# Prompt-only modulation in the first group, a two-pair weight fold, unsaved pooling splits and reductions tied to the heads

## The chip, the cores and the metric

The kernel runs on one core of a Trainium2 chip. The metric is the device time of one execution in microseconds (us); lower is better. The time before is the median of three runs.

TensorE (PE) multiplies matrices; VectorE (DVE), ScalarE (ACT) and GpSimd (POOL) work on vectors; SyncE (SP) issues most transfers. Each engine takes its own instructions strictly in the order of the program, and so an instruction that waits holds up all that stands behind it on its engine.

## The reference

One layer of a streaming encoder, in float32, for a prompt of 2048 tokens and a sample of 64, with the model's width 1024:

```python
mod = (c_act @ w_ada + b_ada)[:, None, :]            # six vectors of 1024, for prompt and sample
sh1, sc1, gt1, sh2, sc2, gt2 = jnp.split(mod, 6, -1)
h = rmsnorm(x, g1) * (1 + sc1) + sh1
proj = h @ w_in                                       # u (pooling), q, k, v, o, gates
pool_out = pool_mixer(u, ...)                         # causal means of 2, 4, 8, 16 rows, then @ w_pool per group
hs, C, n, m = mlstm_seq(q, k, v, ig, lf, C, n, m)     # 4 heads, chunked, state carried from chunk to chunk
hs = hs * rsqrt(mean(hs * hs) + EPS) * g_head * sigmoid(o)
x = x + gt1 * (concat([pool_out, hs]) @ w_out)
h2 = rmsnorm(x, g2) * (1 + sc2) + sh2
up = h2 @ w_up                                        # then a causal convolution, a gate, and w_down
x = x + gt2 * ((silu(g) * a) @ w_down)
```

It returns both outputs and the new states.

## The kernel before

The mixer takes four groups of tokens, called here g0 to g3 (three of 512 and a last of 576 that holds the sample), and runs from 0 to some 760 us; the gated MLP takes the rest, and the change does not touch it.

A product is computed in split arithmetic: a weight and an input are each held as a high and a low part, and three passes (high by high, high by low, low by high) make one product. A weight's split costs one ACT instruction (the high part, L394) and one DVE instruction (the low part, L397). `halves` makes the list of weight units of 128x512 for the heads and the pooling projections: in g0 a unit is loaded raw (256 KB, L373), split, and the split is stored to `hl_kept` in DRAM (512 KB, L402); in g1 to g3 the finished split is loaded (512 KB, L378). The output projection's weights are loaded raw and split in each group.

A group goes through these phases: the V projection (L1129); four heads, each with a product for q, k and the gate (`gemm`, L460) beside which the recurrence of the head before it runs; the pooling projections, called U here (L460 with the same `hl` inputs); and the output projection (L460 with `mx` inputs). A head's recurrence (`lstm`) is a chain over the engines:

- PE expands the gate rows (L1293) and transposes k (L1301); DVE scales it into `kw`; PE multiplies q by k (L1319).
- PE makes the states' products from `kw` (L1334); DVE adds them up (`st`, `SP`).
- PE makes the cells (L1354, L1356); ACT and DVE gather them into `nd`; DVE, ACT and POOL work out a factor `sf` (its power on POOL, L1376); DVE scales `nd` by it.
- `end` transposes `nd` back (L1388), one head later, or for the last head within U.

Small sums over the group's rows (`ssum`) go to PE at L515 and come back through DVE copies into `scr`, which L521 needs. For the next group DVE adds squares of rows (L910).

Between these, background generators are advanced by `tick(i)` at fixed points of `gemm`, the V projection and the drains. Two are of interest. `ada(m)` computes one of the six modulation vectors without PE: for each of 16 pieces of `w_ada` (256 KB each) two DVE reductions (L210), one with the prompt's conditioning vector and one with the sample's; each is followed by a short read of the accumulator. g0 runs `ada(2)` and g1 to g3 run `ada(3)` to `ada(5)`. `weight_sums` loads 1 MB of `w_up`, makes four DVE sums (L849 to L854) and stores 1 MB to `wsum` (L855), which the MLP reads; it runs in g1 to g3. A third, `fold`, runs once, in g0: it multiplies rows of `w_out` by `w_pool` on PE (L887), copies the result (L888) and stores it as `wo_in`.

A scheduler puts the instructions of all these into one order for each engine, going by priorities and its own estimate of durations; `keep_in_program_order` pins an instruction. Transfers go out in SP's order, and a load into a buffer waits there until the buffer's last reader is done.

## Time and profile before

| | |
|---|---|
| median of 3 runs | 2160.68 us (2160.2 to 2161.01) |
| profiled execution | 2162.98 us |
| its span, from first to last instruction | 2161.2 us |
| PE busy | 2139.0 us, 99% |
| DVE, ACT, POOL busy | 1628.4, 1094.3, 248.0 us |
| granted PE clock | 0.999 |

The profiled execution's own time is 1.78 us above its span, and 2.30 us above the median of the runs shown. PE is the bound nearly all the way: what PE waits is the little that is left.

### The profile page before, as it was taken

The numbers are of one execution on the slowest core, as the hardware profiler recorded it, in microseconds if no ns is written. First come the engines' busy times: TensorE is split into PE (matmuls) and PEld (weight loads), VectorE is DVE, ScalarE is ACT, GpSimd is POOL, SyncE is SP. The second block draws the span as 40 slices with busy tenths as digits, with TensorE's granted clock in tenths as the row PEclk, the third lists the DMA queues.
The fourth block names the chain that finished last, engine by engine and source line by source line (L and its number), as shares of the span: only waits on it lengthen the run. The fifth ranks groups of instructions, "written<-read, shape, count | busy, mean of one in ns | idle before, by whom it ended". The sixth has DMA issues, their size and how long they took to land.

```text
span 2161.2 us, 37940 instructions
## 1 busy us (share of the span) xinstructions
PE 2139.0 (99%) x13488; PEld 2039.1 (94%) x13488; DVE 1628.4 (75%) x3068; ACT 1094.3 (51%) x2182; POOL 248.0 (11%) x499
## 2 busy tenths in 40 slices
PE   8999999999999999999999999999999999999998
PEld 7878988888899999999999999999999999999998
DVE  5688768767964868797967668988876597887874
ACT  4554335334333546464636445655655365565554
POOL 0000000002000101010101220100101231111112
PEclk9999999999999999999999999999999999999999
DMA  8897998988886576889967976666668675555552
GB/s 313 318 327 254 326 340 278 357 319 290 282 306 224 169 256 220 305 278 313 341 216 249 322 258 211 230 221 207 220 228 281 209 264 184 176 176 186 175 159 79
DMA packets 245862, 543.63 MB, mean 252 GB/s; under 512 B 25252, under 2 KB 68772, under 8 KB 242856
## 3 DMA queue, kind: packets, MB, share of 16 engines
q1 hardware_dynamic: 236232, 518.89, 70.7%
q10 hardware_dynamic: 9440, 22.32, 2.6%
q8 instruction: 106, 1.74, 0.3%
q14 instruction: 84, 0.69, 0.1%
HBM read 415.12 MB, written 125.99 MB: 250 GB/s over the span
## 4 chain that ended last, share of the span: by engine, by line
PE 78%; DVE 4%; DMA 3%; issue 1%; ACT 1%; SPq 0%; POOL 0%; POOLq 0%; DVEq 0%; ACTq 0%
PE mm L1599 37%; PE mm L460 16%; PE mm L2171 12%; PE mm L2047 9%; PE mm L1129 1%; DVE wt L397 1%; DMA wt<-wsum 1%; DMA raw<-w_ada 1%; DMA wsplit<-wt 1%; PE m L1354 0%; PE m L1356 0%; PE m L1334 0%; DMA wsum<-w 0%; PE m L1319 0%; DMA qs<-w_quad 0%
## 5 line engine op out<-in xcount | busy, mean ns | idle before, releaser
L1599 PE MATMUL mm<-hx,wt 128*128 128x352 f32 x5544 | 885.6, 321 | 1.3 <-DVE eg L1608 0.8
L1599 PEld LDWEIGHTS mm<-hx,wt 128*128 128x128 f32 x5544 | 879.0, 188 | 2.7 <-DVE wt L397 1.4
L460 PE MATMUL mm<-hl,wt 128*128 128x512 f32 (+2 forms) x1920 | 387.6, 357 | 0.2 <-ACT va L233 0.2
L394 ACT ACTIVATE wt<-raw 128x512 fp32r<-128x512 f32 (+3 forms) x470 | 276.9, 597 | 172.6 <-PE mm L2171 50.1
L460 PEld LDWEIGHTS mm<-hl,wt 128*128 128x128 f32 x1920 | 315.0, 189 | 43.0 <-ACT va L233 0.4
L397 DVE TENSOR_TENSOR wt<-raw,wt 128x512 fp32r<-128x512 f32 (+3 forms) x470 | 312.3, 670 | 54.4 <-ACT wt L394 51.9
L2171 PE MATMUL mm<-av,wt 128*128 128x448 f32 (+1 forms) x1632 | 262.7, 322 | 0.0
L2171 PEld LDWEIGHTS mm<-av,wt 128*128 128x128 f32 x1632 | 250.4, 188 | 11.1
L2017 DVE SCALAR_TENSOR_TENSOR x<-mm,MOD,x 128x352 f32<-128x352 f32 (+3 forms) x360 | 167.2, 502 | 78.9 <-PE mm L2171 66.2
L2047 PE MATMUL mm<-av,wt 128*128 128x352 f32 x1344 | 219.7, 323 | 0.9 <-DVE x L2017 0.7
L2047 PEld LDWEIGHTS mm<-av,wt 128*128 128x128 f32 x1344 | 215.3, 188 | 3.2 <-DVE x L2017 1.0
L1646 ACT ACTIVATE mm<-mm 128x352 f32<-128x352 f32 x196 | 87.9, 448 | 239.9 <-PE mm L1599 188.4
L460 PE MATMUL mm<-mx,wt 128*128 128x512 f32 (+1 forms) x960 | 183.0, 352 | 0.3 <-DVE scr L233 0.3
L460 PEld LDWEIGHTS mm<-mx,wt 128*128 128x128 f32 x960 | 159.4, 188 | 23.1 <-issue 0.5
L1577 DVE SCALAR_TENSOR_TENSOR ta<-ea,V,ta 128x704 f32<-128x704 f32 (+1 forms) x132 | 125.6, 952 | 63.3 <-ACT ta L1572 50.6
L1577 DVE SCALAR_TENSOR_TENSOR tg<-eg,V,tg 128x704 f32<-128x704 f32 (+1 forms) x132 | 125.7, 952 | 60.6 <-ACT tg L1572 58.2
L397 DVE TENSOR_TENSOR wt<-wt 128x512 fp32r<-128x512 f32 x196 | 132.5, 682 | 12.7 <-ACT wt L394 12.7
L394 ACT ACTIVATE wt<-wt 128x512 fp32r<-128x512 f32 x196 | 119.9, 623 | 43.4 <-DMA wt<-wsum 33.0
L1555 POOL COPY ea<-UC 128x2 f32<-128x2 f32 x66 | 32.9, 498 | 491.1 <-DVE ta L1577 389.0
L1786 ACT ACTIVATE tg<-tg 128x704 f32<-128x704 f32 (+1 forms) x66 | 52.5, 795 | 71.2 <-DVE tg L1577 71.2
L1129 PE MATMUL mm<-wt,hl 128*128 128x256 f32 (+1 forms) x576 | 71.1, 284 | 0.0
L1129 PEld LDWEIGHTS mm<-wt,hl 128*128 128x128 f32 x576 | 70.3, 190 | 0.6 <-issue 0.4
(298 smaller groups left out, 2169.3 us busy)
## 6 DMA issues: line engine op xcount, KB each, us to landing
wt<-wsplit SPq DMA_DIRECT2D x132, 512.0 KB, 4.4
raw<-w_up SPq DMA_DIRECT2D x198, 256.0 KB, 4.0
wt<-hl_kept SPq DMA_DIRECT2D x96, 512.0 KB, 6.0
wt<-wsum SPq DMA_DIRECT2D x132, 256.0 KB, 4.9
wsplit<-wt SPq DMA_DIRECT2D x66, 512.0 KB, 5.5
w<-w_up SPq DMA_DIRECT2D x44, 512.0 KB, 5.4
wsum<-w SPq DMA_DIRECT2D x22, 1024.0 KB, 4.9
Bd<-fscr ACTq DMA_DIRECT2D x56, 352.0 KB, 4.1
```

Of the source, the lines that this page charges most:

```text
L394: act.activation(u.w[:, 0, :u.n], u.raw[:, :u.n], AF.Copy)
L397: dve.tensor_tensor(out=u.w[:, 1, :u.n], in0=u.raw[:, :u.n], in1=u.w[:, 0, :u.n].bitcast(F32), op=ALU.subtract)
L460: pe.matmul(ps[bi][:, :hi - lo], U[:, a, k % 4 * P:(k % 4 + 1) * P], mv[k][:, b, lo:hi], start=(at == 0 and pi == 0), stop=(k == order[-1] ...
L1129: pe.matmul(ps[ti][:n, :cols], h[4 * kh + k4][:, b, lo:lo + n], U[:, a, k4 % 2 * cols:(k4 % 2 + 1) * cols], start=(kh == 0 and k4 == 0 and ...
L1555: pool.tensor_copy(ext[:, 0:2], UC[:, f, :])
L1577: dve.scalar_tensor_tensor(out=t[:, :E], in0=ext[:, j:j + E], scalar=wc(j, f), in1=t[:, :E], op0=ALU.mult, op1=ALU.add)
L1599: pe.matmul(bk.t[:, :FH], U[:, a, kc * P:(kc + 1) * P], Bo.at(nm, kc, b), start=(first and kc == 0 and pi == 0), stop=(kc == 3 and pi == 2 ...
L1646: act.activation(to.t[:, :FH], bk.t[:, :FH], AF.Copy)
L1786: act.activation(self.tg[:, :E], self.tg[:, :E], AF.Silu)
L2017: dve.scalar_tensor_tensor(out=x3[n][:, a:b], in0=bk.t[:, a - lo:b - lo], scalar=gt2(n, s), in1=x3[n][:, a:b], op0=ALU.mult, op1=ALU.add)
L2047: pe.matmul(bk.t[:, :FH], U[:, a, c:c + P], quad.put(op, m, b), start=(first and m == 0 and pi == 0), stop=(m == 1 and pi == 2), skip_grou ...
L2171: pe.matmul(bks[i].t[:, :hi - lo], U[:, a, k % 4 * P:(k % 4 + 1) * P], av[k][:, b, lo:hi], start=(k == 0 and (a, b) == PASSES[0]), stop=(k ...
```

## The change

Five things, of which the line numbers after the change are some 5 to 20 higher (L460 is L464, L1334 is L1351, L1354 and L1356 are L1372 and L1374, L397 is L400, L849 to L854 are L854 to L859, L515 and L521 are L520 and L526).

- `ada(2)` in g0 makes the prompt's part alone, 16 reductions in place of 32. The 16 of the sample are made in g1, g2 and g3 (6, 6 and 4), behind that group's own `ada`, and the pieces of `w_ada` are loaded again for it. All of `ada`'s reductions are pinned in program order now, where only those of `ada(2)` were.
- From g1 on, `tick(3)`, which advances `ada`, no longer comes in `gemm`, but in the head's recurrence: two steps behind the cells and four behind the scaling of `nd`. In the V projection it moves to the second half.
- `fold` uses two pairs of buffers (one pair are the state tiles `SS` and `SN`, not yet in use), loads two steps ahead, and issues its 8 loads and 8 stores of 256 KB on ACT's queue in place of SP's 4 and 4 of 512 KB.
- The pooling projections' splits are not stored: each group loads their weights raw and splits them, 8 more splits on ACT and on DVE in each of g1 to g3; 8 stores and 24 loads of 512 KB go, 24 loads of 256 KB come.
- In the last head of a group, `end` comes one step later.

```diff
-    def ada(m, quarter=None):
+    def ada(m, quarter=None, ss=(0, 1), bs=range(KD)):
-        todo = [(b, i) for b in range(KD) for i in range(2)]
+        todo = [(b, i) for b in bs for i in range(2)]
...
-        pin = tc.keep_in_program_order if m in (2,) else lambda i: i
+        pin = tc.keep_in_program_order
...
-            for s in range(2):
+            for s in ss:
...
     def halves(key, src, n):
...
+            if key < 4:
+                out.append((src[:, c:c + w], w))
+                continue
...
     def gemm(...):
...
-            if at == 4 and not quiet and not spare:
+            if at == 4 and not quiet and not spare and first_group:
                 tick(3)
...
-        for i in (1, 3):
-            tick(i)
+        tick(1)
+        if first_group:
+            tick(3)
...
         def fold():
+            first = quarter(True)
+            pairs = [[first[:, 0], first[:, 1]],
+                     [t.rearrange("p h c -> p (h c)")[:, :512] for t in (SS, SN)]]
+
+            def load(n):
+                for i, t in enumerate(pairs[n // 2 % 2]):
+                    act.dma_start(out=t, in_=w_out[n + i, :, :512])
+            load(0)
+            load(2)
+            yield
             for n in range(0, KD, 2):
-                w = quarter(True)
-                nc.sync.dma_start(out=w, in_=w_out[n:n + 2, :, :512].rearrange("n p c -> p n c"))
-                yield
-                for i in range(2):
-                    t = w[:, i]
+                for i, t in enumerate(pairs[n // 2 % 2]):
                     ps = m2_ps()
                     for gi in range(4):
                         c = slice(gi * P, (gi + 1) * P)
                         pe.matmul(ps[:, c], WPT[:, c], t[:, c], start=True, stop=True)
                     act.activation(t, ps, AF.Copy)
-                    if i == 0:
-                        yield
-                nc.sync.dma_start(out=wo_in[n:n + 2].rearrange("n p c -> p n c"), in_=w)
-                yield
+                    act.dma_start(out=wo_in[n + i], in_=t)
+                    if i == 0 and 2 <= n < KD - 2:
+                        load(n + 2)
+                    yield
...
-                    if hv == 0 and ti % 2 == 0:
+                    if hv == 1 and ti % 2 == 0:
                         tick(3)
...
+        def steps(o, n):
+            if o.g > 0:
+                for _ in range(n):
+                    tick(3)
         def lstm(o, hd, qko, va, cols, mix):
...
+            steps(o, 2)
...
+            steps(o, 4)
...
-                for _ in range(5 - len(o.segs)):
+                for _ in range(6 - len(o.segs)):
                     yield
                 end()
...
             if o.g > 0:
+                first_group.clear()
                 bg[3].append(ada(2 + o.g))
+                bg[3].append(ada(2, ss=(1,), bs=(None, (0, 1, 2), (3, 4, 5), (6, 7))[o.g]))
+                tick(3)
...
-                    bg[3].append(ada(2, quarter))
+                    bg[3].append(ada(2, quarter, (0,)))
```

Three places show how this moves instructions. A trailing x3 counts like instructions in a row; `m`, `mm` are PSUM tiles, `w` a tile of `weight_sums`, `hl` the group's normalised input, `va` the values, `RHL` the gate rows.

DVE in g2, between head 0 and the `kw` of head 1. Before, the end of the list reads

```order
L850 TENSOR_TENSOR w_4462<-w_4462 128x512
L910 TENSOR_TENSOR ssum<-ssum,mx_4364 128x576
L852 TENSOR_TENSOR w_4462<-w_4462 128x512
L854 TENSOR_TENSOR w_4462<-w_4462 128x512
L910 TENSOR_TENSOR ssum<-ssum,mx_4364 128x576
L233 TENSOR_TENSOR kw<-m_4751,CL 128x512
```

and after the change

```order
L210 ISA raw,MOD<-raw,acc,MOD 128x512
L210 ISA MOD 128x1
L854 TENSOR_TENSOR w_4480<-w_4480 128x512
L855 TENSOR_TENSOR w_4480<-w_4480 128x512
L857 TENSOR_TENSOR w_4480<-w_4480 128x512
L233 TENSOR_TENSOR kw<-m_4761,CL 128x512
```

The reduction at the top is the last of twelve that now stand between this head's cells and the next head's `kw`; before there was one.

PE in g2, from the last cell of head 2 (`m_5016`, later `m_5041`) on. Before:

```order
L1356 MATMUL m_5016<-va,at 128x129
L460 MATMUL mm<-hl_3955,wt 128x512 x3
L460 MATMUL mm<-hl_3731,wt 128x512 x3
L460 MATMUL mm<-hl_3742,wt 128x512 x3
L460 MATMUL mm<-hl_3755,wt 128x512 x3
L460 MATMUL mm<-hl_3804,wt 128x512 x3
L460 MATMUL mm<-hl_3809,wt 128x512 x3
L460 MATMUL mm<-hl_3858,wt 128x512 x3
L460 MATMUL mm<-hl_3905,wt 128x512 x3
L460 MATMUL mm<-hl_3955,wt 128x512 x3
```

After:

```order
L1374 MATMUL m_5041<-va,at 128x129
L464 MATMUL mm<-hl_3981,wt 128x512 x3
L464 MATMUL mm<-hl_3757,wt 128x512 x3
L464 MATMUL mm<-hl_3768,wt 128x512 x3
L464 MATMUL mm<-hl_3781,wt 128x512 x3
L464 MATMUL mm<-hl_3830,wt 128x512 x3
L1309 MATMUL m_5204<-RHL,E_r 128x512
L520 MATMUL m_5169<-ssum,ones_r 32x128 x4
L520 MATMUL m_5169<-ssum,ones_r 32x64
L464 MATMUL mm<-hl_3835,wt 128x512 x3
L464 MATMUL mm<-hl_3884,wt 128x512 x3
L464 MATMUL mm<-hl_3931,wt 128x512 x3
```

The sum over `ssum` now stands 15 products behind that cell; before, the row L515 stood 51 behind it, and from the cell to the states of head 3 there were 60 products, now 39.

PE and DVE in g2 at the start of U. Before, PE passed from the last cells of head 3 (`m_5221`) into products whose weights were split long before:

```order
L1354 MATMUL m_5221<-st_5193,q 128x129
L1356 MATMUL m_5221<-va,at 128x129
L460 MATMUL mm<-hl_3955,wt 128x512 x3
L460 MATMUL mm<-hl_3731,wt 128x512 x3
L460 MATMUL mm<-hl_3742,wt 128x512 x3
```

After the change the next product is U's first, and DVE, whose rows follow, splits its weight only behind the scaling of `nd`:

```order
L464 MATMUL mm<-hl_3931,wt 128x512 x3
L464 MATMUL mm<-hl_3981,wt 128x512 x3
L1374 MATMUL m_5271<-va,at 128x129
L1372 MATMUL m_5275<-st_5244,q 128x129
L1374 MATMUL m_5275<-va,at 128x129
L464 MATMUL mm<-hl_3757,wt 128x512 x3
```

```order
L233 SCALAR_TENSOR_TENSOR nd<-m_5275,CL,nd 128x129
L233 TENSOR_TENSOR sf<-nd 128x4
L233 TENSOR_TENSOR sf<-sf,CL 128x4
L233 SCALAR_TENSOR_TENSOR sf<-sf,sq 128x4
L233 TENSOR_TENSOR nd<-nd,sf 128x4x128
L400 TENSOR_TENSOR wt<-raw,wt 128x512 x5
```

So the first U product reads a weight whose split waits, on DVE, for the last cell that PE made just before it.

More of the change, by code (lines that the diff above doesn't have):

```diff
@@ L195, in load @@
                 got[i] = raw_tile()[:, :512]
-                nc.sync.dma_start(out=got[i], in_=w_ada[m - 2, i])
+                nc.sync.dma_start(out=got[i], in_=w_ada[m - 2, 2 * todo[i][0] + todo[i][1]])
         lead = 4 if quarter else 3
-        pin = tc.keep_in_program_order if m in (2,) else lambda i: i
-        cond = [[a1.tile([P, UE], F32, tag=nm, name=nm)[:, :512] for nm in two] for two in (("u", "s1"), ("s2", "acc"))]
-        for s in range(2):
+        pin = tc.keep_in_program_order
+        cond = {s: [a1.tile([P, UE], F32, tag=nm, name=nm)[:, :512] for nm in (("u", "s1"), ("s2", "acc"))[s]] for s in ss}
+        for s in ss:
             for i in range(2):
@@ L207, in ada @@
             w = got.pop(n)
-            for s in range(2):
+            for s in ss:
                 to = MOD[:, m, b, s:s + 1]
-                pin(dve.tensor_tensor_reduce(out=w if s else junk[0], in0=w, in1=cond[s][i], scale=1.0,
+                pin(dve.tensor_tensor_reduce(out=w if s == ss[-1] else junk[0], in0=w, in1=cond[s][i], scale=1.0,
                                              scalar=to if i else V[:, V_BA + m * 8 + b:V_BA + m * 8 + b + 1],
@@ L262, in tile_layer @@
     stream = []
-    hl_kept = dr.tile([32, P, 2, 512], F32, tag="hl_kept", name="hl_kept")
+    hl_kept = dr.tile([24, P, 2, 512], F32, tag="hl_kept", name="hl_kept")
     place_of = {}
@@ L448, in tile_layer @@
     quiet = []
+    first_group = [1]
     def gemm(ps, W, mv, o, ks=None, order=None, late=None, ups=(1, 3, 4, 6)):
@@ L1321, in lstm @@
                 dve.tensor_tensor(out=at[:n, lo:lo + w], in0=at[:n, lo:lo + w], in1=pq[:n, :w], op=ALU.mult)
+            steps(o, 0)
             while ends:
@@ L1340, in lstm @@
                                              in1=pv[:, ti - a, :], op0=ALU.mult, op1=ALU.add)
+            steps(o, 0)
             extra()
```

## The prediction

> **What bounds it now.** I read the page's busy times and its chain first, then PE's waits within the mixer, then stretches and single rows. The columns of the first row are busy time, share and count; the second gives the shares of the chain that ended last.

> ```profile
> PE 2139.0 (99%) x13488; PEld 2039.1 (94%) x13488; DVE 1628.4 (75%) x3068; ACT 1094.3 (51%) x2182; POOL 248.0 (11%) x499
> PE 78%; DVE 4%; DMA 3%; issue 1%; ACT 1%; SPq 0%; POOL 0%; POOLq 0%; DVEq 0%; ACTq 0%
> ```

> PE is the bound. The change gives it the same multiplications, so the time moves only by what PE stands idle. Of that the mixer has, from 10 to 770 us (line, what it waited for: total, times, longest):

> ```profile
> PE m L1334 <- DVE kw L233: 2.0, 2, 1.8
> PE m L887 <- DMA w<-w_out: 1.9, 2, 1.2
> PE mm L1388 <- DVE nd L233: 1.1, 1, 1.1
> PE m L962 <- ACT scr L960: 0.4, 1, 0.4
> PE m L521 <- ACT scr L233: 0.4, 1, 0.4
> PE mm L460 <- DVE scr L233: 0.3, 1, 0.3
> PE mm L1058 <- ACT hl L983: 0.3, 1, 0.3
> PE mm L460 <- ACT va L233: 0.2, 1, 0.2
> ```

> These are 6.6 us, 0.3% of the time: the most that the change can win, and no pooling projection or kept weight is among them. In the stretch

> ```profile
> 620.00:647.00 27.00, 26.60 (x201) 25.89 (x200) 16.13 (x41) 10.93 (x36) 2.37 (x7) 1.00 0.88 318
> ```

> PE lacks another 0.4 us of 27, in g3. A new wait, on the other hand, costs PE its whole length.

> **The change, part by part.** *The fold.* Both its waits (1.9) are for loads issued a few us ahead of use:

> ```profile
> 99.36 0.38 SPq L880 DMA_DIRECT2D w<-w_out  x1
> 104.05 1.16 PE L887 MATMUL m<-w,WPT 128*128 128x128 f32 x8 [0.74 <-DMA w<-w_out]
> ```

> Issued two steps ahead they land in time: gain 1.9 (0 to 1.9). [...] The 16 issues cost ACT some 0.38 each, 6 us beside its 49% of idle time; two of them wait for a store of the same buffer to land, a few us in which ACT's copies stand still, and PE has products to do: 0.2 (0 to 2).

> *g0's other waits.* Half its reductions leave DVE, and `end` of the last head comes behind 33 products in place of 18, 15 times 0.23 us (below) against a wait of 1.1: gain 1.1, with L521's 0.4 and the lesser `kw` wait of 0.2. The 0.4 of g3 goes with the sums that moved. Together 2.1 (1 to 2.1).

> *Four heads, `kw`.* The other `kw` wait is in g1, between head 0 and 1:

> ```profile
> 265.05 0.39 PE L1356 MATMUL m<-va,at 128*128 128x129 f32 x2
> 265.19 13.19 PE L460 MATMUL mm<-hl,wt 128*128 128x512 f32 x57
> 282.88 1.16 PE L1334 MATMUL m<-va,kw 128*128 128x129 f32 x8 [1.79 <-DVE kw L233]
> ```

> A product takes 13.19/57 = 0.231 us. From the last cell at about 265.3 PE has work until 281.1, and `kw`, 0.69 long, must start by 280.4: 15.1 us after the cell. DVE's list there is priced by these rows:

> ```profile
> 266.63 0.75 DVE L210 CUSTOM_DVE_ANT_0 junk<-raw,s,MOD 128x512 f32<-128x512 f32 x1 [3.02 <-DMA raw<-w_ada]
> 277.39 0.69 DVE L852 TENSOR_TENSOR w<-w 128x512 f32<-128x512 f32 x1
> 278.00 0.69 DVE L910 TENSOR_TENSOR ssum<-ssum,mx 128x512 f32<-128x512 f32 x1
> 279.20 0.74 DVE L210 CUSTOM_DVE_ANT_0 junk<-raw,u,V 128x512 f32<-128x512 f32 x1
> 282.13 0.69 DVE L233 TENSOR_TENSOR kw<-m,CL 128x512 f32<-128x512 f32 x1
> ```

> Four reductions with their reads run from 279.20 to 282.13: 0.73 each. A sum takes 0.61 (277.39 to 278.00). After the cell come some 1.3 for `nd`, 0.5 for `sf`, 0.75 of waiting for POOL and 0.6 for the scaling: 3.15. Before, with 10 reductions and 9 sums, that is 3.15 + 7.3 + 5.5 = 16.0 (the row says 16.9; the late piece of `w_ada` in the first row is the rest). After: 12 reductions and 7 sums in g1 heads 1 and 2, 12 and 6 in g2 head 1, 12 and 5 in g2 head 2, that is 16.2, 16.2, 15.6, 15.0 against 15.1. Waits of 1.1, 1.1, 0.5 and 0.2: 2.9 in place of 1.8. PE's cover is the same 60 products in all four. Bounds: 0 if the lists are 1 us shorter, and 3.0 more if one piece is as late as above.

> *g1, head 3.* The weight of U's first product is split on DVE behind `kw` and two more, four times 0.61, while PE has 1.9 us: 0.5; with a chance of a late reduction, 0.8 (0 to 2). In g3 the heads' cover is 126 shorter products and the lists are no longer than in g1: 0.2 (0 to 1).

> *g2, head 3.* Before, it looks so:

> ```profile
> 485.23 0.39 PE L1356 MATMUL m<-va,at 128*128 128x129 f32 x2
> 485.84 0.87 DVE L233 SCALAR_TENSOR_TENSOR nd<-m,CL,nd 128x129 f32<-128x129 f32 x3 [0.64 <-ACT nd L233]
> 489.22 0.69 DVE L233 TENSOR_TENSOR nd<-nd,sf 128x512 f32<-128x512 f32 x1 [1.19 <-POOL sf L1376]
> 489.83 0.75 DVE L910 TENSOR_TENSOR ssum<-ssum,mx 128x576 f32<-128x576 f32 x1
> 497.13 0.52 PE L515 MATMUL m<-ssum,ones_r 128*32 128x128 f32 x10
> ```

> The last cell ends at 485.5 and `ssum` is complete at 490.6, 5.1 us later; PE asks for it at 497.1. Now PE asks 15 products and one gate row later, 3.7 us. With one sum more in DVE's list, 5.7: a wait of 2.0 (1.4 to 2.5). L526 then needs copies that stand behind four reductions and two sums, 2.9 + 1.2 + 0.4 = 4.5, while PE has 0.5 and 12 products, 3.3: another 1.2 (0.8 to 1.6). Together 3.2.

> *g2, start of U.* The first product's low weight part comes behind the scaling of `nd`, and that behind the cell PE made just before. Before, the same chain ran beside 27 products:

> ```profile
> 507.45 0.39 PE L1356 MATMUL m<-va,at 128*128 128x129 f32 x2
> 507.59 6.40 PE L460 MATMUL mm<-hl,wt 128*128 128x512 f32 x27
> 508.06 0.87 DVE L233 SCALAR_TENSOR_TENSOR nd<-m,CL,nd 128x129 f32<-128x129 f32 x3 [0.64 <-ACT nd L233]
> 509.37 0.71 DVE L233 TENSOR_TENSOR s<-u 128x527 f32<-128x527 f32 x1
> 510.33 1.41 POOL L1376 TENSOR_TENSOR sf<-sf,half 128x4 f32<-128x4 f32 x1 [0.20 <-DVE sf L233]
> 511.77 0.69 DVE L233 TENSOR_TENSOR nd<-nd,sf 128x512 f32<-128x512 f32 x1 [0.91 <-POOL sf L1376]
> 512.99 0.68 DVE L397 TENSOR_TENSOR wt<-raw,wt 128x512 fp32r<-128x512 f32 x1
> ```

> From 507.6 to the end of the scaling 4.9 us, a split of 0.7 on top, less the 0.7 of the row `s<-u`, which no longer stands between: 4.8 (4.1 if that row's follower fell out too, 5.5 if neither did), with nothing for PE to do. This is the largest term. The raw weight itself is no later: SP issues it behind a store of sums and a load of `w_up`, and a raw unit takes

> ```profile
> raw<-w_qkou SPq DMA_DIRECT2D x32, 256.0 KB, 4.8
> wt<-hl_kept SPq DMA_DIRECT2D x96, 512.0 KB, 6.0
> ```

> 4.8 us, within the same wait. The other 23 raw units, 4.6 us of splits a group on DVE and as much on ACT, lie beside U's products: 12 of these, 2.8 us, for a split of 0.6, and the sums of `weight_sums` that waited before find room later in the output projection.

> *Pause and clock.* [...] PE waited 5.7 us at the very start, and the stretch reads a granted clock (third column from the end) of 1.00:

> ```profile
> 0.00:10.00 10.00, 4.27 (x10) 3.48 (x11) 2.85 (x5) 5.40 (x10) 2.26 (x14) 1.00 0.82 294
> ```

> So the sum takes no loss of clock.

> **The sum.** Gains 1.9 + 2.1 + 1.8 = 5.8. Losses 0.2 + 2.9 + 0.8 + 0.2 + 3.2 + 4.8 = 12.1. Net 6.3 slower. The profiled execution took 2162.98, 1.78 above its span; it would take 2169.3. It lies 2.3 above the median, and the median goes from 2160.68 to 2167.0.

> **Rivals.** *No change.* The lists of the four heads are covered (0 in place of 2.9), g1 and g3 lose nothing, and the two chains of g2 take their lower ends, 2.2 and 4.1: 6.3 lost against 5.8, or 2161.2. For it speaks that a late `kw` leaves the next one more time, so that losses in a row need not add up; against it that the U chain can't be shortened much, since its links stand in the rows.

> *Faster.* This one turns on a single mechanism, the start of U in g2. If PE has other work there, by the cells coming some 20 products before the weight is needed, the 4.8 vanish, and with them most of the 3.2, since head 3 then runs as before. With the heads at 0 to 1 the net is 4.5 to 5.5 won: 2155.7. It decides from about 1.5 us of losses on. For it: 20 products stood there in the trace. Against it: the order of the changed kernel puts none.

> *Late pieces.* The reductions are pinned and packed four in a row; their loads come from five raw buffers through SP, which stops for the stores of sums and for the two loads behind them. The row at 266.63 shows 3.0 us of it. Two heads so hit, without slack, give 2167.0 + 4 to 5: 2171.5. Half of the heads have no slack to lose, but the loads are issued earlier than there.

> *The fold stays late.* The cause would be not SP's queue but the transfers: in a stretch that holds fold products the mean busy share of the DMA engines (last column but one) is 0.97.

> ```profile
> 135.00:162.00 27.00, 25.54 (x147) 20.48 (x146) 22.04 (x52) 13.21 (x33) 3.08 (x5) 1.00 0.97 348
> ```

> 1.9 more, 2168.9.

> **How the numbers follow.** About 0.2%, 4.3 us, is what a measurement tells from no change: up to 2156.4 is faster, from 2165.0 on slower. Chances: my sum 0.37 (its own range 2164.5 to 2169.5), no change 0.34, faster 0.15, late pieces 0.09, fold 0.05. The first range reaches a little into no change, as far as that case reaches above 2165. So faster 0.16, same 0.35, slower 0.49. For 8 in 10 the range goes from 2157.0, short of the full gain, to 2171.0.

> **What would show it.** In the profile after, L898 waits for no load, and L1408 not in g0. In g2 PE has one pause of 4 to 5.5 us ended by DVE's `wt` L400 and one of 1 to 3 at L520, before U begins; `kw` waits of 0.2 to 1.1 stand at L1351 in heads 1 and 2. If the U pause is under 2 us, the chain isn't what holds it, and the prediction is wrong by most of its size; if PE's waits in the mixer sum to under 6, the kernel is no slower. A granted clock under 1.00 behind the pause would add to it.

## The result, and the profile after

| | before | after |
|---|---|---|
| median | 2160.85 us (2160.2 to 2163.64) | 2186.87 us (2186.11 to 2190.54) |
| ratio, 95% interval | | 1.0113 [1.0101, 1.0125] |
| span of the profiled execution | 2161.2 us | 2185.4 us |
| PE busy | 2139.0 us | 2149.0 us |
| PE idle within the span | 22.2 us | 36.4 us |
| PE's waits from 10 to 800 us | 6.6 us | 20.6 us |
| granted PE clock | 0.999 | 0.995 |

The change makes the kernel 1.1% slower, 26 us, four times what was forecast; 2186.87 lies outside the range. The span grew by 24.2: PE waits 14.2 more, and it is busy 10.0 more with the same 13488 instructions. The page's busy times and PE's waits in the mixer after the change, in the columns of the lines of before:

```profile
PE 2149.0 (98%) x13488; PEld 2044.0 (94%) x13488; DVE 1639.8 (75%) x3092; ACT 1106.5 (51%) x2206; POOL 252.6 (12%) x499
```

```profile
PE m L1351 <- ACT at L233: 4.8, 1, 4.8
PE mm L464 <- ACT wt L397: 3.5, 1, 3.5
PE mm L1140 <- ACT wt L397: 3.0, 2, 1.6
PE m L520 <- DVE ssum L921: 1.8, 1, 1.8
PE m L1351 <- DVE kw L233: 1.6, 4, 0.5
PE mm L1408 <- DVE nd L233: 1.3, 1, 1.3
PE mm L1140 <- DVE wt L400: 0.7, 3, 0.2
PE m L526 <- DVE scr L521: 0.6, 1, 0.6
```

The waits that the change was to remove are gone: the fold (now L898) waits for no load, L1408 does not wait in g0, and the 1.8 us wait for `kw` in g1 is not there. Three new places take their room, called A, B and C below. At all three ACT splits a raw weight that has only just come; at C that is half of the matter.

**A**, in g0, while the fold runs. PE's row, then ACT's, then SP's (a row of SP is an issue; in brackets the idle time before it and what ended it):

```profile
126.89 2.09 PE L1351 MATMUL m<-va,kw 128*128 128x129 f32 x8 [4.76 <-ACT at L233]
```

```profile
124.65 0.63 ACT L397 ACTIVATE wt<-raw 128x512 fp32r<-128x512 f32 x1 [6.17 <-DMA raw<-w_qkou]
...
125.71 1.12 ACT L233 ACTIVATE at<-m,CL 128x128 f32<-128x128 f32 x4
```

```profile
115.75 4.34 SPq L193 DMA_DIRECT2D w<-w_ada  x4
120.17 0.38 SPq L376 DMA_DIRECT2D raw<-w_qkou  x1
```

PE wants `at`, and ACT makes it behind a split, though PE had ended the products for it (L1335) at 120.1; the split waited 6.17 us for a weight that SP issued at 120.17, behind four loads of `w_ada`. From issue to split 4.5 us passed, no more than the 4.8 that such a load takes in the median, before and after the change. It was issued late; it did not travel slowly.

**B**, in g2's V projection, PE, ACT and SP:

```profile
412.88 0.51 PE L1140 MATMUL mm<-wt,hl 128*128 128x256 f32 x2 [1.60 <-ACT wt L397]
...
415.71 0.50 PE L1140 MATMUL mm<-wt,hl 128*128 128x256 f32 x2 [1.36 <-ACT wt L397]
```

```profile
415.02 0.63 ACT L397 ACTIVATE wt<-raw 128x512 fp32r<-128x512 f32 x1 [1.92 <-DMA raw<-w_v]
```

```profile
404.02 2.44 SPq L196 DMA_DIRECT2D raw<-w_ada  x2
...
410.75 0.33 SPq L376 DMA_DIRECT2D raw<-w_v  x1
```

The weight issued at 410.75 is split at 415.02, 4.3 us later, which is the median of these loads: it too was issued late. The two pieces at 404.02 belong to the group's own `ada`, with two reductions each; the sample's six reductions of g2 run only from 498 to 514 us. So the extra loads do not stand at this place themselves. What they change here is the order that the scheduler made; why it puts this weight so late is not shown.

**C**, in g2 at the start of U:

```profile
522.92 3.10 PE L464 MATMUL mm<-hl,wt 128*128 128x512 f32 x6 [3.54 <-ACT wt L397]
```

```profile
522.24 3.21 ACT L397 ACTIVATE wt<-raw 128x512 fp32r<-128x512 f32 x5 [1.03 <-DMA raw<-w_qkou]
```

```profile
522.60 0.69 DVE L233 TENSOR_TENSOR nd<-nd,sf 128x512 f32<-128x512 f32 x1 [1.19 <-POOL sf L1395]
523.21 3.09 DVE L400 TENSOR_TENSOR wt<-raw,wt 128x512 fp32r<-128x512 f32 x5
```

PE begins at 522.92, before DVE's first low part at 523.21: two of a product's three passes need the high part alone, and that was held for 1.03 us by the raw weight. The third pass needs the low part. In the trace it starts at 523.95, 0.05 us after DVE has made the first, and DVE made that behind the scaling of `nd`. With the raw weight in time two passes would have started about 1 us sooner, and the third at the same time. So the chain that the prediction put here is there, and the late weight stands beside it.

Much of the rest is the clock. Stretches of 4 us at C (the second number is PE's busy time, the third from the end the granted clock):

```profile
520.00:524.00 4.00, 1.08 (x3) 0.55 (x3) 2.32 (x8) 2.86 (x9) 1.54 (x3) 0.81 1.02 392
524.00:528.00 4.00, 4.00 (x13) 3.22 (x13) 3.69 (x7) 2.86 (x6) 0.00 (x0) 0.50 0.73 235
528.00:532.00 4.00, 4.00 (x16) 3.25 (x15) 2.92 (x5) 1.95 (x4) 0.00 (x0) 0.83 0.88 265
```

At clock 0.50 equal products of L464 start 0.43 us apart (from 527.1 to 528.8), at 1.00 0.23 (from 530 on): half of the 4 us from 524 on is lost, and C loses (0.19 + 0.50 + 0.17) × 4 = 3.4 us. A and B lose 1.7 each by the same view (0.82 and 0.75 at A from 124 us on, 0.84 and 0.74 at B from 414 us on): 6.8 us in all, and none in the mixer before. So of the 24.2 us 14.2 are waits and 6.8 clock that followed them. Of the 3.2 more of PE's busy time 1.7 lie behind the mixer, in the MLP that the change does not touch: PE is busy there for 1369.5 us before and 1371.2 after, and for 1368.4 to 1372.1 in the other traces. The last 1.5 are not assigned to a place.

### The profile page after: what moved, and what is told of

It is laid out like the page before. It is cut to its first block, busy times and chain, and to the rows that moved or that the text cites. A ratio compares the mean times of both kernels' runs of the same rounds, so it can differ in the third digit from the quotient of the medians.

```text
span 2185.4 us, 38032 instructions
## 1 busy us (share of the span) xinstructions
PE 2149.0 (98%) x13488; PEld 2044.0 (94%) x13488; DVE 1639.8 (75%) x3092; ACT 1106.5 (51%) x2206; POOL 252.6 (12%) x499
## 3 DMA queue, kind: packets, MB, share of 16 engines
q8 instruction: 106, 1.74, 0.3%
## 4 chain that ended last, share of the span: by engine, by line
PE 68%; DVE 4%; DMA 2%; issue 1%; ACT 1%; SPq 0%; POOL 0%; DVEq 0%; POOLq 0%; ACTq 0%
PE mm L1622 35%; PE mm L2194 11%; PE mm L464 10%; PE mm L2070 9%; PE mm L1140 1%; DVE wt L400 1%; DMA wt<-wsum 1%; DMA wt<-dsum 1%; DVE tg L1600 0%; DMA Bd<-fscr 0%; DMA qs<-w_quad 0%; ACT tg L1595 0%; DMA raw<-w_qkou 0%; PE m L1140 0%; PE m L1351 0%
## 5 line engine op out<-in xcount | busy, mean ns | idle before, releaser
L400 DVE TENSOR_TENSOR wt<-raw,wt 128x512 fp32r<-128x512 f32 (+3 forms) x494 | 328.6, 671 | 84.1 <-ACT wt L397 82.6
L464 PE MATMUL mm<-hl,wt 128*128 128x512 f32 (+2 forms) x1920 | 387.8, 358 | 3.5 <-ACT wt L397 3.5
L397 ACT ACTIVATE wt<-raw 128x512 fp32r<-128x512 f32 (+3 forms) x494 | 291.8, 598 | 194.7 <-PE mm L464 54.8
L464 PEld LDWEIGHTS mm<-hl,wt 128*128 128x128 f32 x1920 | 317.1, 190 | 48.0 <-ACT wt L397 3.7
L464 PE MATMUL mm<-mx,wt 128*128 128x512 f32 (+1 forms) x960 | 183.7, 353 | 0.6 <-DVE scr L233 0.3
L464 PEld LDWEIGHTS mm<-mx,wt 128*128 128x128 f32 x960 | 159.2, 188 | 24.3 <-DVE mx L492 1.1
L400 DVE TENSOR_TENSOR wt<-wt 128x512 fp32r<-128x512 f32 x196 | 132.6, 683 | 12.2 <-ACT wt L397 12.1
L397 ACT ACTIVATE wt<-wt 128x512 fp32r<-128x512 f32 x196 | 119.7, 622 | 42.6 <-DMA wt<-wsum 30.0
## 6 DMA issues: line engine op xcount, KB each, us to landing
wt<-wsplit SPq DMA_DIRECT2D x132, 512.0 KB, 4.3
raw<-w_up SPq DMA_DIRECT2D x198, 256.0 KB, 3.9
wt<-hl_kept SPq DMA_DIRECT2D x72, 512.0 KB, 5.6
wt<-wsum SPq DMA_DIRECT2D x132, 256.0 KB, 4.7
wsplit<-wt SPq DMA_DIRECT2D x66, 512.0 KB, 5.3
w<-w_up SPq DMA_DIRECT2D x44, 512.0 KB, 5.6
```

Of the source, the lines that this page charges most:

```text
L397: act.activation(u.w[:, 0, :u.n], u.raw[:, :u.n], AF.Copy)
L400: dve.tensor_tensor(out=u.w[:, 1, :u.n], in0=u.raw[:, :u.n], in1=u.w[:, 0, :u.n].bitcast(F32), op=ALU.subtract)
L464: pe.matmul(ps[bi][:, :hi - lo], U[:, a, k % 4 * P:(k % 4 + 1) * P], mv[k][:, b, lo:hi], start=(at == 0 and pi == 0), stop=(k == order[-1] ...
```

## The experiments

The theory to begin with: A, B and C are loads issued late, because SP stands at the pieces of `w_ada`, which wait for DVE and for buffers. The rivals: DVE's longer lists, the pooling weights that come raw now, the steps tied to the heads, and for A the fold on ACT's queue. A last question is what a pause costs PE beyond its length. Each time is a median, with its ratio to the kernel before on the same chip; differences between kernels of different chips are taken from these ratios.

**The sample's part back in g0** (`ada_back`): the fold, the splits and the steps stay as changed.

```diff
-                bg[3].append(ada(2, ss=(1,), bs=(None, (0, 1, 2), (3, 4, 5), (6, 7))[o.g]))
-                    bg[3].append(ada(2, quarter, (0,)))
+                    bg[3].append(ada(2, quarter))
```

> The changed kernel with both parts of ada(2) made in the first group again (the fold still on ACT's queue). In the changed kernel PE waits 4.8 us at 122 to 127 us behind ACT, which waits 6.2 us for a raw weight that SP issued behind four loads of w_ada in a row, each waiting for a reduction. Theory (SP stands behind the reductions): with twice the reductions per piece the loads no longer stand four in a row on SP, the wait of 4.8 and the drop of the granted clock behind it (1.7 us) go: about 2180. Rival (the fold's transfers on ACT's queue hold ACT up): the wait stays, 2186 to 2189. A second rival (the transfers are at their limit, and any raw weight there is late): the wait stays too, or moves.

Measured: 2166.52 us, 1.0014 [1.0004, 1.0024]. B and C are gone, and some 21 of the 26 us with them (1.13% less 0.14%), which none of the three cases had. A stays, against the theory:

```profile
PE m L1351 <- ACT scr L233: 3.7, 1, 3.7
```

So the halved reductions in g0 are not what makes A; the sample's part in g1 to g3 is needed for B and C. PE's order in g2 has changed as well. U's first products now come before head 3's last cell, as in the kernel before, while the changed kernel has all of U behind it. Here 33 of U's passes run right behind the last cell, without a wait:

```profile
512.47 7.76 PE L464 MATMUL mm<-hl,wt 128*128 128x512 f32 x33
```

**The fold as before** (`fold_back`): `fold` has the body of the kernel before, all else as changed.

> The changed kernel with the fold as before (one pair of buffers, on SP's queue). By the first theory the run of w_ada loads on SP is broken up by the fold's own transfers to three and two, so that most of the 4.8 us goes, 1.9 us of waits for the fold's loads come back, and the clock's 1.7 go: 2181 to 2184. By the rival (the fold on ACT) all 6.5 go and 1.9 come back: 2182 as well, but then ada_back would not have gained. If neither, 2186 to 2189.

Measured: 2183.44 us, 1.0088 [1.007, 1.0105]. A is gone, B and C stay:

```profile
PE mm L464 <- ACT wt L397: 3.5, 1, 3.5
PE mm L1134 <- ACT wt L397: 3.2, 2, 1.9
```

So A comes from the new fold; the time alone could not have told, since both cases gave about 2182.

**The pooling splits stored again** (`u_kept`).

```diff
-            if key < 4:
-                out.append((src[:, c:c + w], w))
-                continue
```

> The changed kernel with the pooling projections' splits stored in the first group and loaded whole again. In the changed kernel PE waits 3.5 us at 519 to 523 us, at the start of the pooling projections of the third group, for the first raw weight, and the granted clock is 0.81, 0.50 and 0.83 in the three stretches of 4 us from 520 on (3.4 us lost). Theory (the raw weight and its split are late): both go, about 2180. Rival (the pause belongs to the recurrence that the moved reductions delay, and the whole splits, on the same queue, come as late): 2184 to 2188, with a pause of 2 us or more at the same place.

Measured: 2182.16 us, 1.0083 [1.0064, 1.0103], between the two cases and some 6 us under the changed kernel; the trace is of the slowest of its four executions. A and B stay, and at C a wait of 2.7 stays: what comes late now is the finished split from DRAM, which neither ACT nor DVE has to touch.

```profile
PE m L1348 <- ACT at L233: 4.2, 1, 4.2
PE mm L461 <- DMA wt<-hl_kept: 2.7, 1, 2.7
PE mm L1137 <- ACT wt L394: 2.5, 2, 1.7
```

So without a split the load alone, issued late, is enough for most of C: the raw weights are not needed for it. That the chain over DVE plays no part does not follow; `short_sums` below has the chain without a late load.

**The steps where they were** (`ticks_back`): `tick(3)` in `gemm` and in the V projection's first half for all groups, no steps in the recurrence, `end` as before.

```diff
-            if at == 4 and not quiet and not spare and first_group:
+            if at == 4 and not quiet and not spare:
-                    if hv == 1 and ti % 2 == 0:
+                    if hv == 0 and ti % 2 == 0:
-            steps(o, 2)
-            steps(o, 4)
```

> The changed kernel with the steps of ada in gemm and in the first half of the V projection again, and the last head's end as before. Theory: the waits of the third group's V projection (1.6 and 1.4 us at 411 to 416, with a clock of 0.84 and 0.74 behind them, together 5 us) and those of its last head (1.8 and 0.6) come from the reductions' new places and go: 2177 to 2180. Rival (they come from the raw weights alone, whatever the reductions do): under 2 us of change.

Measured: 2180.7 us, 1.0079 [1.0055, 1.0102]. B is gone, and so is C at the start of U. Head 3's sums in g2 wait 3.1 (and 1.3 in g1), and at 475 us, in the heads, a stored split is late, 2.6 (here too U's weights come raw):

```profile
PE m L519 <- DVE ssum L920: 4.4, 2, 3.1
PE mm L464 <- DMA wt<-hl_kept: 2.6, 1, 2.6
```

The steps choose the places where the extra work hurts. With the work in g1 to g3 they cost some 7 us (1.13% less 0.79%), by two intervals that all but touch. A stays, 3.7.

**Both back** (`ada_fold_back`): the sample's part in g0 and the fold as before; the unsaved splits and the steps are what is left of the change.

> The changed kernel with both parts of ada(2) in the first group again and the fold as before; what is left of the change are the unsaved pooling splits and ada's steps tied to the heads. With ada(2) back the waits of the third group went (B at 411 to 416, C at 505 to 523), and with the fold back the 4.8 us at 122 to 127 (A) went. If these two causes are separate, nothing of the 26 us is left: 2158 to 2162, with the fold's own 1.9 us of waits. Rival (any move of instructions in the first group makes PE wait there, A is chance of the order): a wait of 3 us or more by ACT or DVE between 100 and 135 us, 2164 to 2168.

Measured: 2164.7 us, 1.0009 [1.0000, 1.0018]. A, B and C are gone, PE's waits from 10 to 800 us sum to 6.9 (6.6 before), the longest 1.0, and the clock is 0.999.

The unsaved splits, with their 24 further raw loads and 24 splits on each of two engines, and the steps cost at most 0.18%, 4 us, of their own.

**Loads or reductions.** Two kernels take one half each out of the sample's part in g1 to g3. `no_reload` keeps the 16 reductions but makes them on a tile that is there:

```diff
+            elif once and i < len(todo):
+                got[i] = cond[ss[-1]][0]
```

> The changed kernel, in which the 16 sample pieces of ada(2) in the later groups are not loaded: the reductions run on a tile that is there (the sample's second modulation vector is not computed from the weights, that part is left out). The third group's V weights and kept weights share SP and, in part, the five raw buffers with those loads. Theory (queue and buffers): B and C shrink by more than half, 10 us or more: 2172 to 2177, A stays. Rival (DVE's time for the 16 reductions): 2183 to 2187.

`short_sums` keeps the 16 loads and makes the reductions over 8 of the 512 columns:

```diff
+                in0=w[:, :8] if once else w, in1=cond[s][i][:, :8] if once else cond[s][i]
```

> The changed kernel with the loads of the 16 sample pieces kept, but each of their reductions over 8 elements in place of 512 (the sample's second modulation vector is left out in the main). By the theory of queue and buffers B and C stay, 2182 to 2187. By the rival (DVE's time, 16 times 0.65 us, and what waits behind it) they shrink by more than half: 2172 to 2177. In both, A stays.

Measured: 2171.74 us, 1.004 [1.0026, 1.0054], for the first, and 2184.33, 1.0096 [1.008, 1.0112], for the second. PE's longest wait without the loads, and its longest waits with the loads and short reductions:

```profile
PE m L1353 <- ACT at L235: 3.5, 1, 3.5
```

```profile
PE m L1351 <- ACT at L233: 5.1, 1, 5.1
PE mm L1140 <- ACT wt L397: 2.4, 2, 1.5
PE mm L464 <- ACT wt L397: 2.4, 1, 2.4
PE mm L464 <- DVE wt L400: 1.1, 1, 1.1
```

B and C go with the loads and stay with the reductions as good as gone. It takes the 16 loads of 256 KB to make them; the 12 us of DVE's time (16 reductions of 0.73) do not. But at C it is not by arriving late that a load does it. In `short_sums` ACT splits U's first weight at once when it is through with `nd`, and waits for no load; PE waits for ACT, and then for the low part, which DVE makes behind the scaling:

```profile
520.13 2.17 ACT L397 ACTIVATE wt<-raw 128x512 fp32r<-128x512 f32 x4
```

```profile
521.61 0.69 DVE L233 TENSOR_TENSOR nd<-nd,sf 128x512 f32<-128x512 f32 x1 [1.19 <-POOL sf L1395]
522.22 1.89 DVE L400 TENSOR_TENSOR wt<-raw,wt 128x512 fp32r<-128x512 f32 x3
```

The 3.5 us there are the chain of the prediction, with no late weight. What the four kernels with C share (the changed one, `fold_back`, `u_kept`, `short_sums`) is that U's first product stands right behind head 3's last cell; in all the others U begins before that cell, in `no_reload` too. So the loads act on C by the order: with them the scheduler puts all of U behind head 3.

**The pieces on another queue** (`reload_pool`): the same 16 loads into the same raw buffers, issued by POOL.

```diff
-                nc.sync.dma_start(out=got[i], in_=w_ada[m - 2, 2 * todo[i][0] + todo[i][1]])
+                (nc.sync if len(ss) == 2 else nc.gpsimd).dma_start(out=got[i], in_=w_ada[m - 2, 2 * todo[i][0] + todo[i][1]])
```

> The changed kernel with the 16 sample pieces of the later groups loaded through POOL's queue in place of SP's; they still use the five raw buffers and the same bytes. Theory (SP's place: weights stand on SP behind loads that wait for a reduction): B and C shrink by more than half, 2171 to 2178. Rival (the raw buffers, or the transfers themselves): they stay, 2182 to 2188. A stays in both.

Measured: 2181.57 us, 1.008 [1.0067, 1.0093]. The time is at the rival's edge. The waits for V's and U's weights shrink (3.7 to 1.7, 3.5 to 1.4), U begins before head 3's last cell again, A stays (3.4), and a new wait of 4.2 stands at L526, 2.5 of it in g1:

```profile
PE m L526 <- DVE scr L521: 4.2, 2, 2.5
...
PE mm L1140 <- ACT va L233: 1.7, 2, 0.9
...
PE mm L464 <- ACT wt L397: 1.4, 1, 1.4
```

SP's queue is part of the cause and not all of it. Whether the rest is the five raw buffers that the pieces share with the weights, or the order, stays open. Buffers of their own for the pieces were not tried.

**What A needs.** `ada_pool` is `ada_back` with g0's loads of `w_ada` on POOL's queue, out of SP's way, and no longer pinned in order:

```diff
-                        tc.keep_in_program_order(nc.sync.dma_start(out=w[:, d], in_=w_ada[m - 2, i + d]))
+                        nc.gpsimd.dma_start(out=w[:, d], in_=w_ada[m - 2, i + d])
```

> ada_back with the 16 loads of w_ada of the first group issued on POOL's queue in place of SP's. In ada_back PE waits 3.7 us behind an exponential on ACT, which stands behind a weight's split, which waits for a raw weight that SP issued 4 us late since a load of w_ada ahead of it waited for a reduction. Theory (SP's place behind reductions): without these loads on SP the raw weight is early, the wait and its clock drop go: 2158 to 2161. Rival (the transfers are at their limit, 0.98 of the DMA engines' time there): it stays, 2165 to 2168.

`fold_sp` is `ada_back` with the fold's 16 transfers on SP's queue, everything else of the new fold kept:

```diff
-                    act.dma_start(out=t, in_=w_out[n + i, :, :512])
+                    nc.sync.dma_start(out=t, in_=w_out[n + i, :, :512])
-                    act.dma_start(out=wo_in[n + i], in_=t)
+                    nc.sync.dma_start(out=wo_in[n + i], in_=t)
```

> ada_back with the fold's 16 transfers on SP's queue in place of ACT's, and its two pairs of buffers and early loads kept. PE's wait of 3.5 to 5 us at 120 to 128 us (A) stood in every kernel so far that has the fold on ACT and in none of the others. Theory (ACT's queue: ACT stands for the landing of its own stores, and SP for ACT's transfers): A goes, and the fold's loads stay early: about 1 us under the kernel before, ratio 0.999 to 1.0005. Rival (the two pairs of 256 KB, or the order that they bring): a wait of 3 us or more stays there, ratio 1.0015 to 1.003.

Measured: `ada_pool` 2172.38 us, 1.0039 [1.0026, 1.0051], above both cases; A stays, now as 3.9 us of `kw`. SP no longer has those loads, and it waits for the fold's transfers instead; ACT stands still for one of its own stores (its row in the second fence):

```profile
SPq L405 <- DMA SS<-w_out: 4.3, 1, 4.3
SPq L376 <- DMA wo_in<-SS: 3.3, 1, 3.3
```

```profile
109.26 0.63 ACT L919 ACTIVATE mx<-mx 128x512 f32<-128x512 f32 x1 [4.54 <-DMA wo_in<-SS]
```

`fold_sp`: 2162.74 us, 0.9996 [0.9987, 1.0005]. A is gone, and the time is in the theory's range. The fold's loads are not early, though: the longest wait is 2.2 us at L898 for `w_out`, with one half-clock stretch behind it. Two pairs cost nothing against the fold of before, and the longer lead wins nothing on SP; ACT's queue is what costs (0.9996 against the 1.0014 of `ada_back`). Why SP's store of a split (L405) waits for a transfer of the fold, with which it shares no data, no row says.

**The new fold alone in the kernel before** (`fold_alone`).

> The kernel before with the new fold alone. Theory (A belongs to the fold on ACT's queue and needs nothing else of the change): the fold's 1.9 us of waits go, and a wait of 3 us or more comes at 110 to 130 us with a drop of the clock behind it: ratio 1.0015 to 1.003. Rival (A needs the unsaved splits or the moved steps too): no such wait, ratio 0.9985 to 1.0.

Measured: 2167.1 us, 1.0014 [1.0005, 1.0022], some 3 us, just under the theory's range and above the rival's. Its executions at that time record a granted clock of 0.997 or 0.998, where those of the kernel before have 0.998 or 0.999. By both A needs no other part of the change. The one trace of it, of an execution of 7559 us, does not show the wait, so this rests on the time and the clock alone.

**What a pause costs** (`pauses`): the kernel before, in which POOL holds `kw` back for six lengths. PE's, ACT's, DVE's and SP's instructions stand in the same order as before.

```diff
+PAUSE = {(1, 2): 8, (1, 3): 16, (2, 0): 4, (2, 1): 24, (2, 2): 12, (2, 3): 2}
...
+                    pool.tensor_tensor(out=pd[:, :W], in0=pd[:, :W], in1=ow[:, :W], op=ALU.pow)
+                    pool.tensor_tensor(out=kw[:, a, :W], in0=kw[:, a, :W], in1=pd[:, :W], op=ALU.mult)
```

> The kernel before, in which kw passes through four small POOL operations (subtract, add, power, multiply by the 1 that results) in six heads, on 8 and 16 columns in g1's heads 2 and 3 and on 4, 24, 12 and 2 columns in g2's heads 0 to 3; the orders of the other engines are those of before. PE then waits at L1334 in each of these heads, some 0.5 to 6 us, each as long as its POOL chain less the slack of 0.6 to 1.1 us that the rows of before show, and nothing else is late: no raw weight, no reduction, no queue. It asks for the price of a pause alone. The prediction's step (a pause costs its length and no clock): the time rises by the sum of these waits, the granted clock stays 1.00 behind each, PE's busy time stays within 1 us of 2139.0. Clock theory: behind each wait of 2.2 us and more the 4 us that follow show a granted clock of 0.7 to 0.9, PE's busy time grows by 1.5 to 2 us for each of them, and the time rises by the waits and as much again by half; waits under 1.8 us cost their length alone.

Measured: 2184.04 us against 2162.13, 1.0096 [1.0079, 1.0112]: 21.9 us. The six pauses sum to 14.7; PE's waits in the mixer rose from 6.6 to 20.9, by 14.3, since the wait in g1 shrank. PE's busy time rose from 2139.0 to 2146.5. So pauses cost, taken together, one and a half times their length here. Four of the six rows of PE (the others waited 1.85 and 0.95), and the stretches behind three of them:

```profile
331.16 1.16 PE L1343 MATMUL m<-va,kw 128*128 128x129 f32 x8 [3.15 <-POOL ow L1308]
...
447.70 1.08 PE L1343 MATMUL m<-va,kw 128*128 128x129 f32 x6 [1.79 <-POOL ow L1308]
...
474.88 1.38 PE L1343 MATMUL m<-va,kw 128*128 128x129 f32 x8 [4.46 <-POOL ow L1308]
...
500.31 1.16 PE L1343 MATMUL m<-va,kw 128*128 128x129 f32 x8 [2.49 <-POOL ow L1308]
```

```profile
332.00:336.00 4.00, 4.00 (x13) 3.17 (x13) 1.91 (x5) 0.00 (x0) 0.00 (x0) 0.57 0.39 122
...
448.00:452.00 4.00, 4.00 (x15) 3.28 (x15) 3.08 (x9) 0.00 (x0) 0.00 (x0) 0.57 0.40 160
...
500.00:504.00 4.00, 3.69 (x20) 3.21 (x21) 2.54 (x7) 0.00 (x0) 0.28 (x2) 1.00 0.75 262
```

The clock theory holds in kind and in the sum, not in its bound. The clock dropped behind 3.15 and 4.46, but also behind 1.79, and not behind 2.49 or 1.85. Length alone does not decide; the last section has what else was measured.

## Why the prediction was wrong

The direction was right: slower, as the likeliest case had it. The size was wrong, net 6.3 us forecast and 26 measured. The waits account for 14 of them in place of 6.3, and 8.5 of these 14 stand at A and B, where the sum had 0.2. The clock, which the sum left out, accounts for 6.8.

**Pause and clock: this step failed most plainly.** "So the sum takes no loss of clock" rested on the pause at the very start, behind which the column reads 1.00. That was a misreading: the trace's first record of the clock stands at 11.41 us, and the column shows 1.00 where there is none. The row that the prediction shows has ten products in 4.27 us, 0.43 each. PE's rows of one line of the kernel before, up to 11 us and then from 11.65 us on, say the same (count, busy time, mean ns):

```profile
L1021 PE MATMUL m<-mx 128*128 128x256 f32 x12 | 5.5, 648 | 5.7 <-DMA mx<-xT 5.7
```

```profile
L1021 PE MATMUL m<-mx 128*128 128x256 f32 x3 | 0.8, 379 | 0.0
```

They start 0.43 us apart up to 11.0 and 0.22 apart from 11.4 on: PE began at half its clock. Whether the pause or the idle time ahead of the kernel did that, the trace cannot tell. In the mixer, after the change, four intervals at half clock cost 6.8 us, 1.7 each, and `pauses`, which adds nothing but pauses, has three of them. From 100 us on in the mixer, each of the 24 drops of the last section's table stands behind an interval of 3.41 us in which PE was idle for 1.7 us or more.

The other terms of the sum, and what it lacked:

- **The fold on ACT: mis-sized.** 0.2 (0 to 2) was taken, with ACT's idle share as cover. It measured 4.8 at A and 1.7 of clock. The idle share was no cover: what stands behind a held issue on ACT are the weight splits and `at`, for which PE waits. That ACT's queue is needed for A is shown by `fold_sp`. The way from there to A is argued: around it ACT stands 1.94 us for the landing of its own store and SP 3.2 us for ACT's transfers, but the late weight in A's rows also stands behind SP's waits for reductions. The gain of 1.9 came as forecast: L898 waits for no load.
- **g2's V projection: left out.** No term named it; B measured 3.0 + 0.7, and 1.7 of clock. The rival of the late pieces comes nearest, with SP stopping ahead of loads that ACT and PE need, but it put that in the heads and at 4 to 5 us in all.
- **Start of U in g2: right in its chain, a little high.** 4.8 (4.1 to 5.5) forecast, 3.5 measured, plus 3.4 of clock. From the last cell's end at 519.39 to the first low part at 523.90, behind the scaling, 4.5 us pass: that is the forecast chain. The sum did not count that two passes need the high part alone, so that PE starts 1 us earlier and ACT's part ends the wait. "The raw weight itself is no later" is wrong by 1.03 us on ACT, which the chain covers; `short_sums` has 3.5 us there with the weight in time.
- **g2, head 3: right in place, a little high.** 3.2 forecast for L520 and L526, 1.8 + 0.6 measured.
- **Four heads' `kw`: somewhat high.** 2.9 forecast, 1.6 measured in four waits in the four heads named, each 0.5 or less. (The last of the four terms, 0.2, does not follow from its own 15.0 against 15.1.) g1's 1.8 went as forecast.
- **g0's other waits: half right.** L1408 no longer waits in g0, but 1.3 us of it stands in g1 now, at U, where the prediction had 0.8 for a split.
- **The unsaved splits and the steps at nothing: right by themselves.** Without the reloads and the fold on ACT they are worth 0.09% [0.00, 0.18]. Together with the reloads the steps cost some 7 us more (`ticks_back`), which no term had.

How the 26 us, 1.13%, divide by the ratios: 0.99%, 21 us, go with the sample's part in g1 to g3 (`ada_back`), and 0.73%, 16 us, with its loads alone (`no_reload`). The fold on ACT costs, net of its gain, 0.14% alone, 0.18% between `ada_back` and `fold_sp`, 0.25% by `fold_back`: 3 to 5 us. The parts do not add exactly, since each moves the others' places. No version here beats the kernel before; `fold_sp`, which keeps the new fold on SP's queue, equals it.

## What to carry to other kernels

In this kernel, with PE 99% busy, 14.3 us of new waits cost 21.9 (`pauses`). An estimate from its traces is to price a new pause at its length and, where PE's idle time in one interval of 3.4 us comes to 1.7 us or more, at a further 1.7 us of clock: 24 of the 29 such intervals that began at full clock were followed by one at 0.50. Whether another kernel shows the same is for its own traces to say. Before trusting a clock of 1.00, look at how far apart equal products start (here 0.43 us in place of 0.22 under a column of 1.00). ACT's idle share of 49% said little of what 16 DMA issues on its queue cost (4.8 us at A): look at which instructions stand behind the issue and who waits for these, and also whether other queues wait for its transfers. Added loads can cost where they do not stand themselves, by the order that they bring, as at C (3.5 us): compare PE's order before and after at every place where a weight comes just in time, not only in the stage that the change speaks of.

## What the runs showed of the hardware that was not expected

```profile
332.40:332.50 0.10, 0.10 (x2) 0.05 (x1) 0.08 (x1) 0.00 (x0) 0.00 (x0) 0.50 0.01 0
...
335.80:335.90 0.10, 0.10 (x2) 0.09 (x1) 0.00 (x0) 0.00 (x0) 0.00 (x0) 1.00 0.80 205
```

Read so, the drops of `pauses` begin at 332.3, 448.4 and 475.7, those of the changed kernel at 126.6, 416.7 and 522.5. Their distances, 116.1 and 27.3 us and 290.1 and 105.8 us, are whole multiples of 3.413 us (290.1 / 85) as closely as 0.1 us can tell: 34 and 8, and 85 and 31. Every stretch in the mixer lasts 3.4 or 6.8 us at 0.50, and the values of longer windows, 0.57 or 0.75, are mixtures.

PE's idle time in each interval of the grid that began at full clock, summed by PE's rows from 100 us on in the mixer, over the eleven traces that have a drop there (all but `before`, `ada_fold_back` and `fold_alone`):

| idle time in one interval of 3.41 us | clock at 0.50 in the next | at 1.00 |
|---|---|---|
| 2.0 us and more | 16 | 0 |
| 1.7 to 1.9 us | 8 | 5 |
| 0.9 to 1.6 us | 0 | 19 |

Of the 32 intervals at half clock in these traces, the 8 in which PE was idle for 0.43 us or more were followed by a second one; after the other 24, with 0.33 us or less, the clock was full again. C has such a second one: its wait of 3.54 us reaches from 519.39 to 522.92, 0.42 us past the drop at 522.5, and the clock is 0.50 until 529.3.

In `pauses` the 2.49 us, behind which the clock stays at 1.00, are divided by the grid into 1.74 and 0.75. The drop in B, at 416.7, stands behind an interval in which the 1.36 us and smaller gaps come to 1.81. Where the grid lies differs between the profiled executions (drops at 126.6 in the changed kernel, 125.3 in `ada_back`, by other fractions of 3.413); whether the same pause costs the same twice was not measured. What decides between 1.7 and 1.9 stays open: in the changed kernel the interval from 502.0 has 1.81 us of idle time too, and behind it the clock is 1.00. So do the first 20 us: in `ada_back` a stretch at 0.50 begins at 16.1 us behind an interval in which PE stood idle for only 0.2 us, though with small products.
